# The first group of gates in a hybrid encoder block: four turned-sum transfers, one gate product and three scale sums issued at other places

## The chip, the core and the metric

One core of one Trainium2 chip runs the whole layer. The metric is the device time of one execution in microseconds (us), lower is better; the time before is the median of three runs. The core's engines work at the same time and meet through semaphores: PE multiplies matrices, ACT, DVE and POOL work on vectors, and SP issues the transfers.

## The reference

The layer takes 1024 tokens of width 1024. What matters here is how the attention's output and the gates meet:

```
u = RMSNorm(x)
[q|k|v|cB|cC|cH|gA|gB] = u @ W_in
A: 2-D neighbourhood attention, 8 heads x 64
B: cB * conv3(cC * cH)
m = sigmoid(gA) * (A @ W_A) + sigmoid(gB) * (B @ W_B)
x = x + m @ W_o
x = x + relu(RMSNorm(x) @ W1)^2 @ W2
```

The inputs are float32. The kernel splits each operand of a product into two float16 parts, high and low, and adds three products of parts for each one of the reference.

## The kernel before

**Stages.** The program is one straight list of instructions per engine, made by a Python program that writes them in the order in which each engine shall take them. After the norm and the projections to v, q and k comes the attention, a loop over steps `k` of 0 to 79 (lines 1138 to 1180), with the projections of the convolution branch written between its matmuls (`emit`). Then come eight groups of gates (lines 1401 to 1524), then the product with W_o and the MLP.

**Attention.** A step `s` is one head of one block of 128 queries. Its scores come in step `k = s`, its softmax weights P are split into a high and a low part on ACT (line 1085) and DVE (line 1089), and for each pair of heads SP turns P with one transposing DMA into a tile `PT` (`at_turn`, line 1094, issued in step `k = s + 6`). Every eighth step PE multiplies four turned pairs with v (`at_pv`, line 1106). The last of these comes in step 73 and uses the pair that is turned in step 68.

**Gates.** A group of gates is a product of u with 256 columns of W_in, done with one level of Strassen's scheme: seven products of sums of u's quarters (the "forms" 0 to 6) with sums of the weights' quarters. Each product is 12 matmuls of 128x128 weights and 128x512 columns (four blocks times three pairs of parts), so one product counts as 6144 columns in `work`. The pairs of parts come as high times high, high weights times low form, low weights times high form. In this text "product three" is the entry 3 of `SEVEN`, which takes form 6. The forms' sums were computed early and stored to DRAM as `gs`; SP reads them back with transposing DMAs (`turn_one`, line 1133), one for each block `n` of 128 tokens and each part `s`. Forms 4 and 5 go into places of `qD` that the attention no longer reads, and are turned during the attention, at steps listed in `turns`. Form 2 (into `uT`) and form 6 (into `s4T`) follow after the attention loop (line 1209 and on), eight transfers each.

**The first group** (`first_gate`) is written out by hand: gate products 1, 2, 6, 4, 7, 5, 3 with the four products of the two branches (`branch(g, half)`, 12 matmuls each; branch 0 is A, branch 1 is B) between them. A `then` that is handed to `unit` is the work on ACT and DVE after a product; it is written behind the next product's matmuls.

**Weights of a gate group** are made ready one group ahead, by `prep_s(n + 1)` while group `n` runs: rows scaled on ACT (line 1242), squares summed (line 1251), sums of quarters on POOL (line 1256), then one scale for the whole chunk. For this scale PE adds the partitions with one matmul against `ones` (line 201, `all_sum`), DVE makes a power of two out of it in some small instructions (lines 204 and 435 to 442), and ACT (line 1276) and DVE (line 1272) write the high and low parts in four pieces: the quarter 11, the quarters of row 2, and two pieces out of the tile `gsum`. Gate product six of the next group, its second, uses the last of them. How many products PE runs between the sum of squares and the matmul against `ones` is set by the third argument of `scale_of`. In this text "chunk five" is the weights of group five, made ready while group four runs.

**Work between PE products** is written with `tick`, which advances these generators by one step, so a matmul against `ones` that moves also moves the small DVE instructions behind it against the other DVE work.

Of the kernel before, what the change touches and what calls it, by code (L numbers as in the profile page):

```python
# [52 lines left out]
def encoder_block(ctx: ExitStack, tc: tile.TileContext, x, weights, cols, gqk, rel, masks, out):  # L53
# [25 lines left out]
    sc = base.tile([128, 600], F32, name="sc")  # L79
# [41 lines left out]
    def advance(g):  # L121
        try:
            return next(g) or True
        except StopIteration:
            return False

    def step(n=1):
        for _ in range(n):
            for g in list(fg):
                if not advance(g):  # L130
                    fg.remove(g)

    def tick(n=1):

        for _ in range(n):
            i = 0
            while i < len(bg):
                r = advance(bg[i])
                if not r:
                    bg.pop(i)  # L140
                elif r == WAIT and side[0]:
                    i += 1
                else:
                    break
# [3 lines left out]
    def spend(v=0, a=0):  # L148

        debt[0] += v  # L150
        debt[1] += a
# [55 lines left out]
    def unit(mms, post=None, steps=0, ticks=0, free=False):  # L207

        for ps, l, r, a, b in mms:
            T.matmul(ps, l, r, start=a, stop=b, skip_group_check=free)  # L210
        for g in list(hooks):
            if not hold[0] and not advance(g):
                hooks.remove(g)
        units[0] += 1
        work[0] += len(mms) * mms[0][0].shape[-1]
        settle()
        if post:
            late.append(post)
        for i in range(max(steps, ticks)):
            if i < steps:  # L220
                step()
            if i < ticks:
                tick()

    def settle():
        while late:
            late.pop(0)()
# [117 lines left out]
    for (kind, j), pieces in plan():  # L345
        ch = chunks[kind, j] = Chunk(kind, [(nk, sum(n for _, n in cs)) for _, _, nk, cs in pieces],
                                     {"A": "wa", "B": "wb"}.get(kind, "ws"), rows.get(kind, lambda j: g1)(j),
                                     j if kind == "V" else None, 9 if kind in "VQKCS" else 0)
# [115 lines left out]
    def group(ps, pairs):  # L464
        return [(ps, l, r, i == 0, i == len(pairs) - 1) for i, (l, r) in enumerate(pairs)]
# [6 lines left out]
    def ch_mms(ps, act, half, ch, nk, w, c):  # L472

        return group(ps, [(ch.parts[:, sw, k * w + c:k * w + c + 128], act(sa, k)[:, half * 512:half * 512 + 512])
                          for k in range(nk) for sw, sa in PASSES])
# [656 lines left out]
    def turn_one(i, f, n, s):  # L1132
        SP.dma_start_transpose(FORM[f](s)[:, :, 128 * n:128 * n + 128], GS[:, n, (3, 0, 2, 1)[i], s])  # L1133

    turns = {}
    for n in range(8):
        turns[35 + 2 * n] = (1, 4, n // 2, n % 2)
        turns[51 + 2 * n if n < 4 else 65 + 2 * (n - 4)] = (2, 5, n % 4, n // 4)

    def emit(n):  # L1140
        for ps, l, r, a, b in islice(conv, n):
# [3 lines left out]
    for k in range(N + 16):  # L1145
        p, w = k // 16, k % 16
        if p < 3 and w == 3:
            bias[p + 1] = bias_load(p + 1)
        if p < 3 and w in (12, 14):
            bias_make(*bias[p + 1], (w - 12) // 2)  # L1150
            spend(550)
        ok = lambda d: 0 <= k - d < N
        debt[:] = [max(0, v - SPAN) for v in debt]
        spend(1200 if k > 4 else 600, 1120 if k > 3 else 500)
        if ok(0):
            at_qk(k)
        emit(0 if k > 13 and k % 8 == 1 else 4)
        if ok(1):
            at_max(k - 1)
        if ok(4):  # L1160
            at_hi(k - 4)
        if k % 2 and ok(3):
            at_recip(k - 3)
        if ok(5):
            at_lo(k - 5)
        if k % 2 == 0 and ok(6):
            at_turn(k - 6)
        if k in turns:
            turn_one(*turns[k])
        if ok(1):  # L1170
            at_exp(k - 1)
        units[0] += 1
        conv_step(1)
        for _ in range(3):
            if k < 2 or not room() or not fill():
                break
        emit(3 if k < 12 else 0 if k % 8 == 1 else 4 if k % 8 in (3, 5, 7) and k > 16 else 5)
        if k % 8 == 1:
            for d in (17, 15, 13, 11):
                if ok(d):  # L1180
                    at_pv(k - d)
        if ok(14 + k % 2):
            at_out(k - 14 - k % 2, k % 2)
# [16 lines left out]
    p3 = ExitStack()  # L1200
# [25 lines left out]
    def scale_of(am, more, n=3, lag=1):  # L1226

        a, mark = am
        yield from apart(mark, n * 6144, work)
        b, s, inv = cols_of("prep", 1), cols_of("prep", 1), keep()  # L1230
        yield from all_sum(a, b, anybank(), 1e-36, lag)
        yield from pow2_half(b, 14, s, inv, more)
        return s, inv
# [11 lines left out]
    def forms_sum(ch, t, gap):  # L1245

        sm = cols_of("prep", 2)
        for i in range(2):
            while len(ch.raw) <= i:
                yield WAIT  # L1250
            A.activation(t[:, 2:4].rearrange("p a c -> p (a c)"), ch.raw[i], AF.Square, accum_out=sc[:, at(sm, i)])
            yield
        ch.r = [ch.raw[i].rearrange("p (n m) -> p n m", n=2) for i in range(2)]
        (w11, w12), (w21, w22) = ([r[:, 0], r[:, 1]] for r in ch.r)
        for o, a, b in ((0, w11, w12), (1, w12, w22), (2, t[:, 0], w22), (3, t[:, 2], w21)):
            G.tensor_tensor(t[:, o], a, b, op=OP.add)  # L1256
        yield from apart(work[0], gap * 6144, work)
        ch.sum = sum_of(sm)
        yield
# [30 lines left out]
    def prep_s(n):  # L1290

        ch = cS[n]
        t = w3p.tile([128, 4, 512], F32, name="gsum", bufs=1)
        yield from rows_scaled(ch, g1)
        yield from forms_sum(ch, t, 2 - 0 * (n % 2 == 0))
        s, ch.inv = yield from scale_of(ch.sum, 9, 2 + 1*(n % 2 == 0), 0)
        hold[0] = True
        while done[0] < ch.first:
            yield WAIT
        ch.P = wsp.tile([128, 7, 2, 512], F16, name="w16_s", tag="ws")  # L1300
        yield from forms_split(ch, t, s, ch.P)
        ch.split = True
        hold[0] = False
# [82 lines left out]
    def first_gate(post):  # L1386

        sg = w3p.tile([128, 4, 512], F32, name="sg")
        z = [sg[:, i] for i in range(4)]
        P, iv, ps = cS[0].P, cS[0].inv, {}  # L1390

        def op(o, a, b, less=False):
            V.tensor_tensor(z[o], ps[a], z[b], op=OP.subtract if less else OP.add)

        def sigmoid(i):
            A.activation(z[i], z[i], AF.Sigmoid, scale=sc[:, iv])

        def p6():
            op(1, 6, 1)

        def p2():
            op(0, 2, 1)
            sigmoid(0)

        def p7():
            op(3, 7, 1)
            op(2, 4, 3)
            sigmoid(2)

        def p5():  # L1410
            op(3, 5, 3, True)
            sigmoid(3)
            op(1, 5, 1, True)

        def p3():
            op(1, 3, 1)
            sigmoid(1)

        def gate_of(i, then=None):
            f, w = SEVEN[i]  # L1420
            ps[i] = anybank()
            unit(group(ps[i], [(P[:, w, sw, k * 128:k * 128 + 128], actS(f, sa, k))
                               for k in range(4) for sw, sa in PASSES]), then, 2, 4)

        def branch(g, half):
            ch, act = ((cA[0], actA), (cB[0], actB))[g]
            built(ch)
            bk = anybank()
            unit(ch_mms(bk, act, half, ch, 4, 256, 0), lambda: post(g, half, bk, sc[:, ch.inv], sg), 2, 4)

        gate_of(1, lambda: A.activation(z[1], ps[1], AF.Copy))
        gate_of(2, p2)
        gate_of(6, p6)
        gate_of(4)
        branch(0, 0)
        gate_of(7, p7)
        branch(0, 1)
        gate_of(5, p5)
        branch(1, 1)
        gate_of(3, p3)  # L1440
        branch(1, 0)

    def branch_units(n, post):
        j, cc = n // 2, (n % 2) * 128
# [7 lines left out]
    for n in range(8):  # L1452
# [5 lines left out]
        if n < 7:  # L1458
            sg = gate_units(n) if n else None
# [7 lines left out]
            def post(g, half, ps, iv, sg=sg, m=m):  # L1467
                t = sg[:, 2 * half + g]
                V.scalar_tensor_tensor(t, ps, iv, t, op0=OP.mult, op1=OP.mult)
                if g == 1:  # L1470
                    V.tensor_tensor(m[:, half], sg[:, 2 * half], t, op=OP.add)
# [629 lines left out]
    later = {}  # L2101
# [147 lines left out]
    for n in range(28):  # L2249
        s, o = n // 7, n % 7  # L2250
# [3 lines left out]
        for j in range(4):  # L2254
            bk = anybank()
# [87 lines left out]
```

## Time and profile before

| what | value |
|---|---|
| runs of before | 1196.51, 1197.23 and 1197.74 us, median 1197.23 |
| the profiled execution's own time | 1197.15 us |
| its span on the core | 1195.2 us |
| granted clock of PE, mean | 0.999 |
| PE busy | 1183.5 us, 99% of the span |
| DVE busy | 966.6 us, 81% |
| ACT busy | 760.6 us, 64% |
| POOL busy | 416.2 us, 35% |

The span is the time between the first and the last instruction of the execution; 1197.15 - 1195.2 = 1.95 us of the profiled time lie outside it. In the timeline a row gives its start in us, its length, the engine, the line of the program, the operation, the tiles it writes and reads, how many instructions it merges (x), and in brackets the idle time of the engine ahead of it with what ended it. Matmuls overlap in the records, by some 0.16 us, so the step from the start of one product to the start of the next is what PE spends on it.

### The profile page before, as it was taken

To read this page: it belongs to the slowest core of one execution; us is meant where nothing else is said; L and a number is where in the kernel's file an instruction comes from. 1 tells how busy PE (TensorE), PEld (TensorE's weight loads), DVE (VectorE), ACT (ScalarE), POOL (GpSimd) and SP (SyncE) were. 2 spreads that over 40 slices of the span, in tenths; PEclk is the share of its full clock that TensorE was granted. 3 is DMA by queue.
4 is the path that set the end of the run, shared out by engine and by line. 5 is a ranking of instruction groups with operands and counts; after the bars stand their busy time and mean duration, and the time that the engine had idled before them with its cause. 6 is when DMAs were issued, how large, how long until landed. Compare 5 with 4: busy or idle time off the path is not lost.

```text
span 1195.2 us, 16991 instructions
## 1 busy us (share of the span) xinstructions
PE 1183.5 (99%) x6253; PEld 579.5 (48%) x6253; DVE 966.6 (81%) x1665; ACT 760.6 (64%) x1181; POOL 416.2 (35%) x288
## 2 busy tenths in 40 slices
PE   8999999999999999999999999999999999999998
PEld 6444445555444444444467445555444444444444
DVE  6799888899668686868886867766749899998997
ACT  7866578786657776436766576666686743646440
POOL 2640012224321222001012475776873431324193
PEclk9999999999999999999999999999999999999999
DMA  9949457766625454233364444533675927244302
GB/s 291 217 158 205 114 126 138 141 149 108 188 83 184 150 176 141 89 144 138 87 153 148 161 176 176 193 129 133 207 255 202 375 74 259 94 142 192 106 36 106
DMA packets 181283, 189.61 MB, mean 159 GB/s; under 512 B 138192, under 2 KB 138704, under 8 KB 177104
## 3 DMA queue, kind: packets, MB, share of 16 engines
q1 hardware_dynamic: 181200, 188.52, 52.1%
q8 instruction: 49, 0.80, 0.3%
q14 instruction: 34, 0.28, 0.1%
HBM read 117.19 MB, written 37.75 MB: 130 GB/s over the span
## 4 chain that ended last, share of the span: by engine, by line
PE 57%; issue 6%; POOL 5%; DMA 4%; DVE 2%; ACT 1%; SPq 1%; DVEq 0%; POOLq 0%; ACTq 0%
PE ps_s L210 21%; PE ps_d L210 21%; PE ps_o L210 14%; POOL tsum L1651 3%; DMA hs<-as 3%; POOL as L1539 2%; SPq L1133 1%; PE ps_d L1142 1%; DVE w L1272 1%; DVE as L1989 0%; ACT raw L1642 0%; ACT as L1912 0%; DMA PT<-P 0%; ACT w L1276 0%; DMA s4T<-gs 0%
## 5 line engine op out<-in xcount | busy, mean ns | idle before, releaser
L210 PEld LDWEIGHTS <-ops 128*128 128x128 f16 x1356 | 132.5, 98 | 157.3
L210 PEld LDWEIGHTS <-w 128*128 128x128 f16 x1272 | 124.3, 98 | 127.1 <-issue 0.2
L1142 PE MATMUL ps_d<-uT,w_ws 128*128 128x512 f16 x528 | 123.7, 379 | 0.0
L210 PE MATMUL ps_d<-ops 128*128 128x512 f16 (+1 forms) x540 | 121.0, 374 | 0.0
L1539 POOL TENSOR_TENSOR as<-as 128x512 f32<-128x512 f32 x56 | 92.0, 1644 | 73.8 <-ACT as L1914 70.8
L210 PE MATMUL ps_s<-ops 128*128 128x512 f16 x504 | 115.6, 379 | 0.0
L2166 ACT ACTIVATE ops<-hf,sc 128x2048 f16<-128x2048 f32 x26 | 52.0, 2000 | 86.0 <-PE ps_d L210 37.5
L210 PEld LDWEIGHTS <-w_s 128*128 128x128 f16 x672 | 65.3, 98 | 79.0 <-issue 0.9
L210 PEld LDWEIGHTS <-uT 128*128 128x128 f16 x528 | 51.4, 98 | 62.0
L1651 POOL TENSOR_TENSOR tsum<-raw 128x512 f32<-128x512 f32 x28 | 40.5, 1463 | 114.7 <-ACT raw L1642 114.7
L1142 PEld LDWEIGHTS <-w_ws 128*128 128x128 f16 x528 | 51.4, 98 | 54.2
L210 PE MATMUL ps_o<-ops 128*128 128x512 f16 x312 | 71.6, 379 | 0.0
L2168 DVE SCALAR_TENSOR_TENSOR ops<-hf,sc,ops 128x2048 f16<-128x2048 f32 x26 | 68.0, 2617 | 3.6 <-ACT ops L2166 3.5
L1256 POOL TENSOR_TENSOR gsum<-raw 128x512 f32<-128x512 f32 x14 | 18.6, 1338 | 125.8 <-ACT raw L1242 125.8
L1272 DVE SCALAR_TENSOR_TENSOR w<-tsum,sc,w 128x1024 f16<-128x1024 f32 x28 | 46.8, 1679 | 14.5 <-ACT w L1276 14.5
L210 PE MATMUL ps_d<-u2T,w 128*128 128x512 f16 (+1 forms) x276 | 58.2, 360 | 0.0
L210 PE MATMUL ps_s<-u2T,w 128*128 128x512 f16 (+1 forms) x252 | 54.0, 364 | 0.0
L1272 DVE SCALAR_TENSOR_TENSOR w<-raw,sc,w 128x1024 f16<-128x1024 f32 (+1 forms) x20 | 28.2, 1418 | 31.7 <-ACT w L1276 31.7
L1072 ACT ACTIVATE sz<-sz,sc 128x384 f32<-128x384 f32 (+1 forms) x64 | 37.2, 581 | 24.3 <-DVE sc L1063 15.8
L1912 ACT ACTIVATE as<-as 128x2048 f32<-128x2048 f32 (+1 forms) x18 | 30.9, 1718 | 31.3 <-DVE as L1989 18.8
L309 ACT ACTIVATE w_ws<-raw,sc 128x512 f16<-128x512 f32 (+1 forms) x64 | 37.2, 654 | 18.2 <-DVE sc L282 18.2
L210 PE MATMUL ps_s<-u2x,w 128*128 128x512 f16 (+1 forms) x228 | 48.5, 362 | 0.0
(430 smaller groups left out, 2692.2 us busy)
## 6 DMA issues: line engine op xcount, KB each, us to landing
raw<-in_weights SPq DMA_DIRECT2D x97, 512.0 KB, 4.8
hs<-as SPq DMA_DIRECT2D x16, 1792.0 KB, 8.3
hf<-hs SPq DMA_DIRECT2D x26, 1024.0 KB, 5.9
w2x<-in_weights SPq DMA_DIRECT2D x16, 512.0 KB, 7.0
raw<-in_weights SPq DMA_DIRECT2D x16, 384.0 KB, 4.0
mL<-in_weights SPq DMA_DIRECT2D x10, 512.0 KB, 4.7
mH<-in_weights SPq DMA_DIRECT2D x9, 512.0 KB, 4.3
xt<-in_x SPq DMA_DIRECT2D x8, 512.0 KB, 8.2
```

The lines of the kernel that those rows point to most:

```text
L210: T.matmul(ps, l, r, start=a, stop=b, skip_group_check=free)
L309: A.activation(self.parts[:, 0, f + o:f + o + m], self.raw[p][:, o:o + m], AF.Copy, scale=sc[:, c:c + 1])
L1072: A.activation(z, z, AF.Exp, scale=-1.0, bias=sc[:, d["mx"]], accum_out=sc[:, d["sm"]])
L1133: SP.dma_start_transpose(FORM[f](s)[:, :, 128 * n:128 * n + 128], GS[:, n, (3, 0, 2, 1)[i], s])
L1142: T.matmul(ps, l, r, start=a, stop=b)
L1256: G.tensor_tensor(t[:, o], a, b, op=OP.add)
L1272: V.scalar_tensor_tensor(o(1), w, sc[:, s], o(0), op0=OP.mult, op1=OP.subtract)
L1539: sub.tensor_tensor(z[o], z[a], z[b], op=op)
L1651: G.tensor_tensor(t[:, o], a, b, op=OP.add)
L1912: A.activation(v[:, 0:4], v[:, 0:4], AF.Relu)
L2166: A.activation(P[:, 1, 0], hf, AF.Copy, scale=sc[:, Rs])
L2168: V.scalar_tensor_tensor(P[:, 1, 1], hf, sc[:, Rs], P[:, 1, 0], op0=OP.mult, op1=OP.subtract)
```

## The change

```diff
     turns = {}
     for n in range(8):
-        turns[35 + 2 * n] = (1, 4, n // 2, n % 2)
-        turns[51 + 2 * n if n < 4 else 65 + 2 * (n - 4)] = (2, 5, n % 4, n // 4)
+        turns.setdefault(35 + 2 * n, []).append((1, 4, n // 2, n % 2))
+        turns.setdefault(51 + 2 * n if n < 4 else (65, 65, 69, 70)[n - 4], []).append((2, 5, n % 4, n // 4))
...
-        if k in turns:
-            turn_one(*turns[k])
+        for tn in turns.get(k, ()):
+            turn_one(*tn)
...
-        yield from forms_sum(ch, t, 2 - 0 * (n % 2 == 0))
-        s, ch.inv = yield from scale_of(ch.sum, 9, 2 + 1*(n % 2 == 0), 0)
+        yield from forms_sum(ch, t, 2 - 0 * (n != 3))
+        s, ch.inv = yield from scale_of(ch.sum, 9, 2 + 1*(n != 3), 0)
...
-        def branch(g, half):
+        def branch(g, half, later=None):
             ch, act = ((cA[0], actA), (cB[0], actB))[g]
             built(ch)
             bk = anybank()
-            unit(ch_mms(bk, act, half, ch, 4, 256, 0), lambda: post(g, half, bk, sc[:, ch.inv], sg), 2, 4)
+            fin = lambda: post(g, half, bk, sc[:, ch.inv], sg)
+            unit(ch_mms(bk, act, half, ch, 4, 256, 0), None if later else fin, 2, 4)
+            return fin
...
         branch(1, 1)
-        gate_of(3, p3)
-        branch(1, 0)
+        fin = branch(1, 0, True)
+        gate_of(3, lambda: (p3(), fin()))
```

There are three edits. The last four transfers of form 5 were issued in steps 65, 67, 69 and 71 and are now issued in steps 65, 65, 69 and 70. In the first group, product three now stands behind the last branch product, and that branch product's own work on DVE stands behind product three's. In `prep_s` the distance from the squares to the matmul against `ones` becomes three products for chunks one, five and seven, where it was two; chunk three keeps two, and the even chunks keep three. The edit of the argument of `forms_sum` multiplies by 0 and changes nothing.

On SP, at the end of the attention, the difference reads as follows; `P_3219` is the pair of step 60, `P_3314` (now `P_3315`) the last pair, and the `qD` rows are transfers of form 5.

```order
 L1094 DMA_TRANSPOSE PT<-P_3126 128x12x128
 L1094 DMA_TRANSPOSE PT<-P_3175 128x12x128
-L1133 DMA_TRANSPOSE qD<-gs 128x4x128
+L1133 DMA_TRANSPOSE qD<-gs 128x4x128 x2
 L1094 DMA_TRANSPOSE PT<-P_3219 128x12x128
-L1133 DMA_TRANSPOSE qD<-gs 128x4x128
-L1094 DMA_TRANSPOSE PT<-P_3314 128x8x128
+L1094 DMA_TRANSPOSE PT<-P_3315 128x8x128
 L1133 DMA_TRANSPOSE qD<-gs 128x4x128 x2
 L1133 DMA_TRANSPOSE uT<-gs 128x4x128 x4
```

One form-5 transfer moves from between the last two turned P to ahead of both. Everything behind the last P keeps its order, and the number of transfers is the same.

On PE, behind the first branch-B product (`ps_o<-bT`), before:

```order
L210 LDWEIGHTS w_wb
L210 MATMUL ps_o<-bT,w_wb 128x512
L210 LDWEIGHTS w_s
L210 MATMUL ps_d<-s4T,w_s 128x512
L210 LDWEIGHTS w_s
```

and now, at the same place:

```order
L210 LDWEIGHTS w_wb
L210 MATMUL ps_o<-bT,w_wb 128x512
L210 LDWEIGHTS w_wb
L210 MATMUL ps_d<-bT,w_wb 128x512
L210 LDWEIGHTS w_wb
```

The first reading of `s4T` on PE comes 12 matmuls later. Further ahead on PE, chunk one's matmul against `ones` moves from the front to the back of the second branch-A product.

On DVE, while group four runs, from the scale of chunk five to the last low parts of its weights, before (line 1469 scales a branch product, line 1471 adds two):

```order
L204 TENSOR_SCALAR sc<-ps_o 128x1
L435 TENSOR_SCALAR sc<-sc 128x1
L437 TENSOR_SCALAR sc<-sc 128x1
L1469 SCALAR_TENSOR_TENSOR sg<-ps_s,sc,sg 128x512
L439 TENSOR_SCALAR sc<-sc 128x1
L441 TENSOR_SCALAR sc<-sc 128x1
L442 TENSOR_SCALAR sc<-sc 128x1
L1272 SCALAR_TENSOR_TENSOR w_s<-raw,sc,w_s 128x512
L1469 SCALAR_TENSOR_TENSOR sg<-ps_d,sc,sg 128x512
L1272 SCALAR_TENSOR_TENSOR w_s<-raw,sc,w_s 128x2x512
L1272 SCALAR_TENSOR_TENSOR w_s<-gsum,sc,w_s 128x2x512 x2
```

and now (the two lines are 1471 and 1473 in the changed kernel, and the first branch product's scaling stands ahead of these rows):

```order
L204 TENSOR_SCALAR sc<-ps_d 128x1
L435 TENSOR_SCALAR sc<-sc 128x1
L437 TENSOR_SCALAR sc<-sc 128x1
L1471 SCALAR_TENSOR_TENSOR sg<-ps_o,sc,sg 128x512
L439 TENSOR_SCALAR sc<-sc 128x1
L441 TENSOR_SCALAR sc<-sc 128x1
L442 TENSOR_SCALAR sc<-sc 128x1
L1272 SCALAR_TENSOR_TENSOR w_s<-raw,sc,w_s 128x512
L1471 SCALAR_TENSOR_TENSOR sg<-ps_s,sc,sg 128x512
L1473 TENSOR_TENSOR m<-sg 128x512
L1272 SCALAR_TENSOR_TENSOR w_s<-raw,sc,w_s 128x2x512
L1272 SCALAR_TENSOR_TENSOR w_s<-gsum,sc,w_s 128x2x512 x2
```

The chunk's scale waits for one branch product more, and the third branch product's scaling and sum now stand ahead of the last three pieces of the split.

## The prediction, made before the changed kernel ran

> **What bounds the kernel now.** I read the waits of PE first, then the busy time by window, then the timelines of PE, SP and DVE around the change. The waits of PE (engine, line, tile, what it waited for, us, times, longest) are five rows in all; the first stands at the very start of the program, the second in the change's region:
>
> ```profile
> PE ps_o L574 <- DMA xt<-in_x: 4.6, 1, 4.6
> PE ps_o L1106 <- DMA PT<-P: 1.2, 1, 1.2
> ```
>
> The busy time by window (PE is the column behind the comma) says how little is left: 1.86 us are idle in one window and 0.55 in the next.
>
> ```profile
> 250.00:300.00 50.00, 48.14 (x459) 26.04 (x458) 46.14 (x114) 35.48 (x81) 19.41 (x21) 1.00 0.71 131
> 300.00:350.00 50.00, 49.45 (x232) 22.27 (x231) 31.72 (x76) 28.20 (x49) 14.38 (x13) 1.00 0.43 127
> ```
>
> So PE sets the end, and a change pays only by what it takes from PE's gaps. The timeline of PE shows three of them:
>
> ```profile
> 299.04 0.53 PE L1106 MATMUL ps_o<-PT,vT 128*64 128x128 f16 x12 [1.21 <-DMA PT<-P]
> 299.50 2.76 PE L210 MATMUL ps_s<-uT,w_s 128*128 128x512 f16 x12
> ...
> 309.87 0.17 PE L201 MATMUL ps_d<-ones 128*128 128x1 bf16 x1
> ...
> 315.36 0.16 PE L201 MATMUL ps_s<-ones 128*128 128x1 bf16 x1
> ...
> 323.15 0.38 PE L210 MATMUL ps_d<-s4T,w_s 128*128 128x512 f16 x1
> 323.95 2.53 PE L210 MATMUL ps_d<-s4T,w_s 128*128 128x512 f16 x11 [0.43 <-DMA s4T<-gs]
> 326.32 1.03 PE L210 MATMUL ps_s<-bT,w_wb 128*128 128x512 f16 x4
> ```
>
> A product takes (309.87 - 299.50) / 4 = 2.59 us, a matmul 0.216. First gap: 1.21 us ahead of the last turned P, which PE wanted at 299.04 - 1.21 = 297.83. Second: from the one matmul against ones to the next are 5.49 us for two products, 5.49 - 5.18 - 0.03 (the matmul itself) = 0.28 too many. Third: product three takes 326.32 - 323.15 = 3.17, 0.58 too many; it waits behind its first matmul for the low part of s4T. All that can be won here is 1.21 + 0.28 + 0.58 = 2.07 us.
>
> **The transfers.** SP and the two low parts of P that release its last turns on DVE:
>
> ```profile
> 288.35 1.98 SPq L1133 DMA_TRANSPOSE qD<-gs  x1
> 292.00 1.45 SPq L1094 DMA_TRANSPOSE PT<-P  x1
> 293.52 1.62 SPq L1133 DMA_TRANSPOSE qD<-gs  x1
> 295.25 1.24 SPq L1094 DMA_TRANSPOSE PT<-P  x1
> ...
> 299.22 5.76 SPq L1133 DMA_TRANSPOSE uT<-gs  x4
> ...
> 311.94 10.38 SPq L1133 DMA_TRANSPOSE s4T<-gs  x8
> ```
>
> ```profile
> 291.02 0.61 DVE L1089 SCALAR_TENSOR_TENSOR P<-sz,sc,P 128x384 f16<-128x384 f32 x1
> ...
> 292.74 0.87 DVE L1089 SCALAR_TENSOR_TENSOR P<-sz,sc,P 128x256 f16<-128x256 f32 x2
> ```
>
> SP stood idle from 288.35 + 1.98 = 290.33 to 292.00, until P came (291.63 on DVE, 0.37 later SP). The moved transfer fits there: issued at 290.4, it takes 1.62 by the nearest row, at most 1.98, and is off SP by 292.0 to 292.4. The turn of step 60 slips by 0 to 0.4. The last turn needs its P at 292.74 + 0.87 = 293.61, so it goes at 293.61 + 0.37 = 293.98 in place of 295.25: 1.27 earlier. From issue to landing (medians of two narrow windows, and the last s4T transfer in the chain of waits):
>
> ```profile
> PT<-P SPq DMA_TRANSPOSE x1, 3.7
> ...
> PT<-P SPq DMA_TRANSPOSE x1, 4.6
> ...
> 321.06 2.75 DMA s4T<-gs
> ```
>
> 3.7 is that very transfer, so it lands at 297.7, when PE wants it: I take the gap as closed. By 4.6, the other row, it lands at 298.6 and 0.4 of the gap is won. But PE does not keep 1.21. Its next meeting is the matmul against ones for the first branch-B weights, whose operand DVE makes here:
>
> ```profile
> 308.92 0.16 DVE L331 CAST ones<-sc 128x1 bf16<-128x1 f32 x1
> ...
> 315.14 0.16 DVE L1223 CAST ones<-sc 128x1 bf16<-128x1 f32 x1
> ```
>
> The cast ends at 309.08, and the second shows what a wait costs: ending at 315.30, it let PE go at 315.36. DVE's work before 308.92 hangs on the convolution's tail, not on PE's products, and its order is unchanged. PE would be there at 309.87 - 1.21 = 308.66 and now waits until 309.14. Of the first gap remain 309.87 - 309.14 = **0.73 us** (bounds 0 and 1.21).
>
> **The matmul against ones of chunk one** moves behind the second branch-A product, 2.59 later, where its cast of 315.30 is long done: **0.28 us** won (bounds 0 and 0.28). Behind it, DVE's split of chunk one comes later; the row of its last low part and the chain's row of the product that reads it:
>
> ```profile
> 326.77 1.28 DVE L1272 SCALAR_TENSOR_TENSOR w_s<-gsum,sc,w_s 128x1024 f16<-128x1024 f32 x1
> ...
> 331.67 2.59 PE ps_d L210 x12
> ```
>
> The high-by-high and high-by-low matmuls come first, so the low part is wanted 0.43 after 331.67. It ends at 328.05: 4.05 to spare. PE comes 1.6 earlier and DVE up to 2.59 later if nothing else moves, which would be 0.1 late; but two of the posts that stood between the pieces now stand behind them, and the loads on SP and so the squares come about 1.3 earlier. I take 0.
>
> **Product three** is read 2.59 later on PE, about 325.74 - 1.01 = 324.73, while the last s4T transfer landed at 323.81 even where it stood, and SP, solid from 299.22 on, now runs 1.3 ahead. The whole **0.58** is won (bounds 0.43, the wait that the row names, and 0.58). The branch product's post stands behind product three's; DVE does both as before. That costs nothing, since product six of the next group only needs the split.
>
> **Chunk five**, with the same later matmul against ones, has no such room. PE, DVE, ACT and POOL while group four runs, and one sum (line 1471) away from POOL:
>
> ```profile
> 435.28 0.17 PE L201 MATMUL ps_o<-ones 128*128 128x1 bf16 x1
> ...
> 445.67 1.67 PE L210 MATMUL ps_o<-qD,w_s 128*128 128x512 f16 x7
> ```
>
> ```profile
> 435.52 0.16 DVE L204 TENSOR_SCALAR sc<-ps_o 128x1 f32<-128x1 f32 x1 [0.45 <-PE ps_o L201]
> ...
> 437.13 0.75 DVE L1469 SCALAR_TENSOR_TENSOR sg<-ps_s,sc,sg 128x512 f32<-128x512 f32 x1 [1.08 <-ACT sg L1347]
> 437.80 0.14 DVE L439 TENSOR_SCALAR sc<-sc 128x1 int32<-128x1 int32 x1
> 437.98 0.15 DVE L441 TENSOR_SCALAR sc<-sc 128x1 int32<-128x1 int32 x1
> ...
> 438.92 0.75 DVE L1272 SCALAR_TENSOR_TENSOR w_s<-raw,sc,w_s 128x512 f16<-128x512 f32 x1 [0.73 <-ACT w_s L1276]
> ...
> 440.25 1.28 DVE L1272 SCALAR_TENSOR_TENSOR w_s<-raw,sc,w_s 128x1024 f16<-128x1024 f32 x1
> 441.44 2.48 DVE L1272 SCALAR_TENSOR_TENSOR w_s<-gsum,sc,w_s 128x1024 f16<-128x1024 f32 x2
> ...
> 444.62 1.26 DVE L1471 TENSOR_TENSOR m<-sg 128x512 f32<-128x512 f32 x1
> ...
> 501.69 0.69 DVE L1471 TENSOR_TENSOR m<-sg 128x512 f32<-128x512 f32 x1
> ```
>
> ```profile
> 438.17 1.76 ACT L1276 ACTIVATE w_s<-raw,sc 128x512 f16<-128x512 f32 x2
> ...
> 444.05 2.96 POOL L1256 TENSOR_TENSOR gsum<-raw 128x512 f32<-128x512 f32 x2 [23.22 <-ACT raw L1242]
> ```
>
> Before, the split ends at 441.44 + 2.48 = 443.92, and its last low part is wanted at 445.67 + 0.43 = 446.10: 2.18 to spare. Now, in times of this trace: the matmul at 437.87, DVE's first step 0.24 later at 438.11, two steps of 0.19, the post (0.67 by 437.13 to 437.80), the step to the scale (0.18): 439.41, against 437.98. ACT starts 0.19 behind it, DVE's first low part 0.75 behind that, at 440.35. Then come 0.67, the third branch product's post and sum, 0.78 (as 1471 follows 1469 elsewhere) and 0.61, the three low parts with 1.19 + 2.48: 446.08. That meets the 446.10 with nothing left; with the hand-over of 0.06 and a weight load I take a stall of **0.15** (bounds 0 and 2.3). For the upper one the whole 2.59 and a post and sum of 0.67 + 1.26 are late, 4.52 - 2.18. The sum is short, 0.61, only because it now stands ahead of POOL's additions, which start when the split frees gsum (444.05 behind 443.92); beside them it took 1.26 against 0.69.
>
> The Trainium skill, GPSIMD Engine Reference, section Specifications, says that POOL shares its SBUF interfaces with DVE and that DVE instructions with two SBUF inputs contend with it; the two rows of line 1471 agree (1.26 against 0.69).
>
> Chunk seven's weights come into use behind four more products of the last group, 10.4 us, so its 2.6 lie in cover.
>
> Sum against the profiled 1197.15: 0.73 + 0.28 + 0.58 - 0.15 = 1.44, so 1195.7; the median of the runs lies 0.08 higher: **1195.8 us**.
>
> **The rivals.** (1) The cast is no bound, or DVE reaches it sooner: 2.07 - 0.15 = 1.92 won, 1195.3. For it: DVE is idle several times before 308.92; against it: those idles end with POOL and ACT work of the convolution. (2) The last turn, now close behind other transfers, lands by the row of 4.6: 0.4 + 0.28 + 0.58 - 0.15 = 1.1 won, 1196.1; for it the spread of 3.7 to 4.6, against it that fewer transfers are in flight ahead of it than before.
>
> The Trainium skill, DMA: Bandwidth & Descriptors, section Issuing engines are not separate DMA queues, says that all transfers end on the same 16 engines and interleave there, so two issued together would delay each other; this is the second rival, and the rows of 3.7 and 4.6 bear it out in part.
>
> (3) The other side: chunk five's split is late by more than I count, at product six of group five. From a stall of 1.6 on it eats everything; with 2.3, 1197.23 - 1.59 + 2.34 = 1198.0, and if its last three pieces run beside POOL at the ratio 1.26 / 0.69, 3 us more, 1201. For it: nothing to spare in my sum; against it: POOL waits for the split's end. (4) The change doesn't do what it says: the last turn still goes at 295.25, since its P or the moved transfer is late. Then 0.28 + 0.58 - 0.15 = 0.71, 1196.5.
>
> **How the numbers follow.** Forecast 0.52, rival (1) 0.16, (2) 0.14, (3) 0.14, (4) 0.04. A change of 0.2%, 2.4 us, is about what a measurement can tell from none. More than that is won only with all gaps closed and luck in the runs, which differ by 1.2: half of rival (1) and 0.06 of the forecast, 0.14. Slower by it is most of (3), 0.10. The rest, 0.76, is within. The range goes from 1194.7 (rival (1) with 0.6 of spread) to 1197.6 (the mild end of rival (3)); the forecast's own is 1195.2 to 1196.4.
>
> **What would show it.** Right: no wait of PE on PT or s4T; the wait at the branch-B matmul against ones, some 0.5 us; product one of group one at 327.3 in place of 328.91; a gap of 0.1 to 0.3 in product six of group five, behind its second matmul. Wrong: PE's next products still 1.2 ahead behind the cast, a gap of 1 us or more in group five or in product six of group one, or any new wait of PE elsewhere.

## The result and the profile after

The changed kernel takes 1195.72 us (median of 22 runs, 1195.15 to 1196.58), the kernel before beside it 1197.43 us (22 runs, 1196.51 to 1199.52). The ratio is 0.9986, with a 95% interval of 0.998 to 0.9992. So 1.7 us are won, a gain that the interval tells from none, and less than the 0.2% that the prediction counts as a change. The profiled execution took 1195.5 us, its span is 1193.4 us.

The waits of PE after the change (engine, line, tile, what it waited for; us in total, times, longest):

```profile
PE ps_o L574 <- DMA xt<-in_x: 4.5, 1, 4.5
PE ps_s L1049 <- DVE sc L1063: 0.7, 2, 0.5
PE ps_d L201 <- DVE ones L331: 0.5, 1, 0.5
...
PE ps_d L546 <- DVE ones L609: 0.2, 1, 0.2
```

The wait for `PT` is gone and no wait for `s4T` is there. A new one of 0.5 us stands at a matmul against `ones`, for the cast of line 331. The row of 0.2 us at line 546, also new, stands at the very start of the program, where the executions scatter (last section). The windows of before, now (PE busy behind the comma):

```profile
250.00:300.00 50.00, 49.34 (x466) 26.56 (x464) 46.13 (x114) 35.49 (x81) 19.41 (x21) 1.00 0.74 134
300.00:350.00 50.00, 49.50 (x233) 22.33 (x232) 32.28 (x77) 29.95 (x51) 14.41 (x13) 1.00 0.44 124
```

The first window gains 49.34 - 48.14 = 1.20 us of work, the second only 0.05: gaps have closed in it, but the new wait at 309 stands in it too. The timeline of PE tells more:

```profile
285.58 2.03 PE L1106 MATMUL ps_o<-PT,vT 128*64 128x128 f16 x66
...
296.07 2.03 PE L1106 MATMUL ps_o<-PT,vT 128*64 128x128 f16 x66
...
305.81 2.75 PE L210 MATMUL ps_s<-uT,w_s 128*128 128x512 f16 x12
309.06 0.18 PE L201 MATMUL ps_d<-ones 128*128 128x1 bf16 x1 [0.50 <-DVE ones L331]
...
314.28 2.75 PE L210 MATMUL ps_s<-qD,w_wa 128*128 128x512 f16 x12
316.87 0.17 PE L201 MATMUL ps_d<-ones 128*128 128x1 bf16 x1
...
324.67 2.75 PE L210 MATMUL ps_s<-s4T,w_s 128*128 128x512 f16 x12
327.26 2.75 PE L210 MATMUL ps_o<-uT,w_s 128*128 128x512 f16 x12
```

The 66 value matmuls run without a stop, and product three (`s4T`) takes one step of 2.59. The only long step is the one ahead of the branch's matmul against `ones`: 309.06 - 305.81 = 3.25, which is 0.66 too many.

The **stretch** that the rest of this text measures goes from the value products of step 65 (285.58) to product one of group one (327.26). It is 41.68 us, and was 328.91 - 285.64 = 43.27: 1.59 us less. Behind it, to PE's last group, nothing is won. These are that group's rows, before and after:

```profile
1188.01 2.78 PE L210 MATMUL ps_d<-ops 128*128 128x256 f16 x24
```

```profile
1186.39 2.78 PE L210 MATMUL ps_d<-ops 128*128 128x256 f16 x24
```

From product one of group one to there are 859.10 us before and 859.13 after. SP and the two casts on DVE, after:

```profile
292.01 3.14 SPq L1094 DMA_TRANSPOSE PT<-P  x2
...
303.90 1.47 SPq L237 DMA_DIRECT2D raw<-in_weights  x3
...
310.73 10.38 SPq L1133 DMA_TRANSPOSE s4T<-gs  x8
```

```profile
308.85 0.16 DVE L331 CAST ones<-sc 128x1 bf16<-128x1 f32 x1
...
313.83 0.16 DVE L1223 CAST ones<-sc 128x1 bf16<-128x1 f32 x1
```

The two turned P now go out together, and all behind them on SP runs 1.2 us sooner: `s4T` at 310.73 in place of 311.94, chunk one's weights (`raw`) at 303.90 in place of 305.09 (the row of before is shown further below). The cast of the branch weights stands where it stood, 308.85 against 308.92.

### The profile page after: what moved, and what is told of

It is laid out like the page before. It is cut to its first block, busy times and chain, and to the rows that moved or that the text cites. A ratio compares the mean times of both kernels' runs of the same rounds, so it can differ in the third digit from the quotient of the medians.

```text
span 1193.4 us, 16991 instructions
## 1 busy us (share of the span) xinstructions
PE 1183.0 (99%) x6253; PEld 579.1 (49%) x6253; DVE 965.9 (81%) x1665; ACT 760.7 (64%) x1181; POOL 416.3 (35%) x288
## 4 chain that ended last, share of the span: by engine, by line
PE 71%; DVE 3%; issue 1%; POOL 1%; ACT 1%; DVEq 0%; POOLq 0%; ACTq 0%
PE ps_s L210 27%; PE ps_d L210 26%; PE ps_o L210 19%; POOL tsum L1653 1%; DVE P L1089 1%; POOL cv L908 0%; DVE w L1272 0%; DVE sz L1063 0%; DVE as L1991 0%; DVE w_wa L300 0%; DVE sc L320 0%; ACT w L1276 0%; ACT as L1914 0%; POOL z L905 0%; DVE cv L891 0%
```

## The experiments

Seven more kernels ran, four of them twice, and the changed kernel once more: twelve runs, each with one trace (the expectations call a trace a look). Where no number of runs is given, the time is of a single execution. Single times do not tell the parts apart, since executions of one kernel differ by 1 us and more. What tells them apart is the stretch and where it is longer than the bare work. The bare work is 41.00 us: one of the kernels below ran the stretch without any gap. Gaps are read from the steps between PE rows, as above, so they are a little longer than the waits in brackets: the wait for the last turned P is 1.21 in its bracket, but takes 1.40 out of PE's steps. All traces, in us; a "sum" stands for the matmul against `ones` of the weights named, and "landing" goes from the first issue of chunk one's weights on SP to ScalarE's start on them:

| kernel | last turned P | branch-B sum | chunk one's sum | product three | stretch | landing |
|---|---|---|---|---|---|---|
| before | 1.40 | 0 | 0.28 | 0.58 | 43.27 | 3.83 |
| the change | 0 | 0.66 | 0 | 0 | 41.68 | 3.70 |
| the change, again | 0.07 | 0.62 | 0 | 0 | 41.70 | 3.75 |
| turns alone | 0.01 | 0.63 | 0.66 | 0.08 | 42.39 | 4.42 |
| product three alone | 1.08 | 0 | 1.38 | 0 | 43.47 | 4.55 |
| the same, again | 0.86 | 0 | 0.54 | 0 | 42.41 | 4.02 |
| sums alone | 1.07 | 0 | 0 | 1.52 | 43.59 | 4.07 |
| the same, again | 1.01 | 0 | 0 | 1.56 | 43.57 | 4.06 |
| turns and product three | 0.25 | 0.41 | 0.43 | 0 | 42.09 | 4.26 |
| the same, again | 0.01 | 0.68 | 0 | 0 | 41.70 | 3.89 |
| the change, cast early | 0.33 | 0 | 0 | 0 | 41.33 | 4.12 |
| the same, again | 0 | 0 | 0 | 0 | 41.00 | 4.13 |

The two kernels that change only the sums of chunks five and three have the stretch of the whole change, 41.68 and 41.70, with landings of 4.29 and 4.02.

### The turns alone

```diff
-        turns[51 + 2 * n if n < 4 else 65 + 2 * (n - 4)] = (2, 5, n % 4, n // 4)
+        turns.setdefault(51 + 2 * n if n < 4 else (65, 65, 69, 70)[n - 4], []).append((2, 5, n % 4, n // 4))
```

Expected:

> Of the change only the moved transfers of form 5. Read on PE: the distance from the start of step 65's value products to the start of product one of group one, 43.27 us before, 41.68 in the changed kernel. Theory (each gap has its own cause, and the loads that follow the transfers on SP also pull the cast of 315.30 forward): first gap 0.5 in place of 1.21, seen at the branch-B matmul against ones; second gap closed although its matmul is not moved; product three waits some 0.3 for s4T, which lands 1.27 earlier while PE comes 1.01 earlier. Distance 42.0. Rival (the second gap needs its matmul moved): 0.2 to 0.3 stay ahead of chunk one's matmul against ones, and product three waits about as much less.

It took 1196.2 us. PE's rows at the two matmuls against `ones` and at product three:

```profile
309.08 0.18 PE L201 MATMUL ps_d<-ones 128*128 128x1 bf16 x1 [0.46 <-DVE ones L331]
...
311.70 2.75 PE L210 MATMUL ps_d<-qD,w_s 128*128 128x512 f16 x12
314.95 0.16 PE L201 MATMUL ps_s<-ones 128*128 128x1 bf16 x1 [0.49 <-DVE ones L1223]
...
322.74 2.83 PE L210 MATMUL ps_d<-s4T,w_s 128*128 128x512 f16 x12
325.41 2.75 PE L210 MATMUL ps_s<-bT,w_wb 128*128 128x512 f16 x12
```

The wait for P is gone and 0.63 of it comes back at the branch's cast, as the prediction had it. On SP, the last transfers that product three needs:

```profile
311.01 10.38 SPq L1133 DMA_TRANSPOSE s4T<-gs  x8
```

Two things were not expected. Chunk one's sum lost 0.66, although its weights were issued 1.0 us sooner than before (304.09 against 305.09). They landed later: 4.42 us from issue to use in place of 3.83. And product three, left where it was, loses only 325.41 - 322.74 - 2.59 = 0.08. That is not the turns' doing alone: PE came to it 0.66 later than it would have without the loss at the sum. What is left waits for the last transfers of `s4T`. In the three traces whose rows show PE waiting for them (the kernel before and the sums alone), product three's second matmul starts 11.97 to 12.05 us behind the first issue of `s4T` on SP (323.95 - 311.94 = 12.01 before). Here this issue comes 25.40 us behind the value products of step 65, and 26.30 before. So the stretch is 0.88 shorter because `s4T` goes out 0.90 sooner, where 1.27 was expected of both; by this reading, a punctual sum would only have made PE wait 0.7 at product three.

### Product three alone

```diff
-        gate_of(3, p3)
-        branch(1, 0)
+        fin = branch(1, 0, True)
+        gate_of(3, lambda: (p3(), fin()))
```

(`branch` also gets its argument `later` from the change.) Expected, first run:

> Of the change only product three behind the last branch product. Theory: product three's gap of 0.58 goes, the other two stay: 1.21 ahead of the last turned P and 0.28 ahead of chunk one's matmul against ones. Distance 42.69 in place of 43.27. Rival (the branch product's work on DVE, now behind product three's, delays group one): 43.0 or more, with a wait of PE in group one.

It took 1197.52 us, and the stretch was 0.20 longer than before, not 0.58 shorter. Product three has no gap. The loss is at chunk one's sum, which this edit does not touch. ScalarE's first row on chunk one's weights, and PE's, in this kernel:

```profile
309.90 1.70 ACT L1242 ACTIVATE raw<-raw,sc 128x256 f32<-128x256 f32 x4 [2.97 <-DMA raw<-in_weights]
```

```profile
316.33 0.16 PE L201 MATMUL ps_s<-ones 128*128 128x1 bf16 x1 [1.22 <-DVE ones L1223]
```

and the same for the kernel before, SP first:

```profile
305.09 1.47 SPq L237 DMA_DIRECT2D raw<-in_weights  x3
```

```profile
308.92 1.70 ACT L1242 ACTIVATE raw<-raw,sc 128x256 f32<-128x256 f32 x4 [2.16 <-DMA raw<-in_weights]
```

The loads go out at 305.35 here and are used at 309.90, 4.55 later, against 3.83 before. The whole chain behind (squares, cast, matmul against `ones`) moves with them. Of the 1.38 - 0.28 = 1.10 that the gap has grown, 0.72 is this; most of the rest is that PE lost less at the last turned P (1.08 in place of 1.40) and so came sooner. Whether the late landing was chance could only be told by a second run:

> Product three behind the last branch product, alone, once more. Theory: the move does take product three out of the landing of s4T (0.58), and what the first look lost again was chunk one's weights, which landed late by chance: the wait at chunk one's matmul against ones is about the time from the first issue of these loads to ScalarE's start, less 3.5 (0.28 at 3.83 before, 1.22 at 4.55). The stretch from step 65's value products to product one of group one (43.27 before) is then 42.7 if that time is 3.8, and 43.4 if it is 4.5. Rival: the move is worth nothing whatever the landing, and the stretch is 43.3 or more even at 3.8.

This time the landing is 4.02, the gap at chunk one's sum 0.54 and the stretch 42.41, below the 42.7 to 43.4 that were expected and 0.86 shorter than before: 0.58 at product three, 0.54 at the last turned P (0.86 in place of 1.40), which this edit does not touch, less 0.26 at chunk one's sum (0.54 in place of 0.28). Over 11 runs the median is 1197.32 us, the ratio 0.9995 (0.9986 to 1.0004). So the edit does take the 0.58 out at product three in both traces, but what the execution as a whole gains is no more than the scatter of the two landings ahead of it.

### The sums alone

```diff
-        s, ch.inv = yield from scale_of(ch.sum, 9, 2 + 1*(n % 2 == 0), 0)
+        s, ch.inv = yield from scale_of(ch.sum, 9, 2 + 1*(n != 3), 0)
```

Expected, first run:

> Of the change only the later matmuls against ones of chunks one, five and seven. Theory: 0.28 is won ahead of chunk one's matmul and given back at product three, whose s4T lands when it did: its gap grows from 0.58 to 0.86. Distance 43.27 as before, no gain. Product six of group five loses 0.02 to 0.05. Rival (the parts simply add up): 42.99.

It took 1197.53 us. Chunk one's sum has no gap, but product three has:

```profile
319.88 2.75 PE L210 MATMUL ps_o<-bT,w_wb 128*128 128x512 f16 x12
322.95 0.38 PE L210 MATMUL ps_d<-s4T,w_s 128*128 128x512 f16 x1 [0.32 <-issue]
324.21 2.53 PE L210 MATMUL ps_d<-s4T,w_s 128*128 128x512 f16 x11 [0.88 <-DMA s4T<-gs]
326.58 2.75 PE L210 MATMUL ps_s<-bT,w_wb 128*128 128x512 f16 x12
```

The two steps around it are 3.07 and 3.63, together 1.52 too many, where 0.58 were before. PE is sooner at product three by the 0.28 that it no longer waits at the sum and by 0.33 that it waits less at the last turned P. It then waits for `s4T` instead, whose issue on SP (312.16) comes no sooner than before: 26.58 us behind the value products, against 26.30.

```profile
312.16 10.38 SPq L1133 DMA_TRANSPOSE s4T<-gs  x8
```

Second run:

> The sums later, alone, once more. Theory: the wait at chunk one's matmul against ones is gone, but what it gives up goes into the wait for s4T at product three, which comes earlier by as much (0.58 before, 1.2 in the first look); the stretch stays at 43.1 to 43.6, and the time at 1197.4 to 1197.7, ratio 0.9995 to 1.0005. Rival: without the other two edits the term of 0.28 is there all the same: stretch 43.0 or less and ratio 0.9993 or less.

Again 1.56 at product three, stretch 43.57, median 1197.49 us, ratio 0.9998 (0.9989 to 1.0007). The theory holds: alone, this edit wins nothing. Product six of group five takes 2.62 and 2.63 in the two traces, against 2.59 before, so 0.03 to 0.04 are lost there, as expected.

### Turns and product three, without the sums

This kernel is the change with the old argument of `scale_of`. Expected, first run:

> The change without the later matmuls against ones: transfers and product three alone. Theory: all of the change's gain, since the earlier loads already take chunk one's cast out of PE's way: distance 41.7, no gap of 0.1 or more ahead of chunk one's matmul, and no loss in product six of group five. Rival: 0.28 missing, 41.96.

1197.64 us; 1.6 of it were lost ahead of the stretch, which starts at 287.20 in place of 285.58 (more on that below). The stretch is 42.09, neither the 41.7 of the theory nor quite the 41.96 of its rival: chunk one's sum lost 0.43 at a landing of 4.26. Second run:

> Turns and product three, without the sums, once more. Theory: all three waits of before are gone except the one at chunk one's matmul against ones, and that is the time from the first issue of chunk one's loads to ScalarE's start less 3.85 (0.42 at 4.26 in the first look), none where they land in 3.7: the stretch is 41.7 at 3.7 and 42.4 at 4.55, and the median over many executions 0.2 to 0.5 above the whole change, 1196.0 to 1196.3. Rival: the sums are worth nothing, 41.7 and 1195.8.

```profile
309.60 0.18 PE L201 MATMUL ps_d<-ones 128*128 128x1 bf16 x1 [0.52 <-DVE ones L331]
...
314.81 0.17 PE L201 MATMUL ps_s<-ones 128*128 128x1 bf16 x1
```

At a landing of 3.89 chunk one's sum costs nothing at all, and the stretch is 41.70, the same as with the whole change. The formula for the single trace holds (3.89 less 3.85), but the forecast for the median does not: 1195.80 us over 11 runs, ratio 0.9987 (0.9978 to 0.9996), so no 0.2 to 0.5 above the whole change. In the median nothing is left for the sums that these runs could show. What they buy is that chunk one's sum had no gap in any of the 8 traces that have them, while it had 0, 0.43 and 0.66 in the three that have the turns without them.

### The branch's cast ahead of the splits

If 0.66 us is left at the branch's matmul against `ones`, and its cast on DVE stands behind four splits of other weights, the cast can go first. Two more steps of its generator are taken, and one more product lies in between so that PE's order stays as it is (ScalarE makes one copy later, behind chunk one's scaling):

```diff
-            yield from apart(units[0], 3 if self.kind != "O" else 1 + (self is cO[1]))
+            yield from apart(units[0], 4 if self is cB[0] else 3 if self.kind != "O" else 1 + (self is cO[1]))
...
+    for _ in range(2):
+        advance(bg[-1])
```

Expected, first run and second:

> The change, and with it the three small VectorE instructions that end in the cast of the branch's second sum (L102, L329, L331) ahead of the four w_wa splits (L300) instead of behind them. If what is left of the first gap is this cast alone (0.50 at the branch's matmul against ones), that wait is gone, the stretch of the PE from step 65's value products to product one of group one (43.27 before, 41.68 with the change) is 41.1 to 41.3, and the time is about 1195.2, ratio to before about 0.9982. Rival: the gap is shut by something else next (the sum's own readiness, chunk one's cast), the stretch stays at 41.6 to 41.8 and the time at 1195.7.

> The change with the branch's cast ahead of the splits, once more. Theory: the wait of 0.5 at the branch's matmul against ones is gone in every execution, so the ratio to before is 0.9978 again to 0.0005 and the stretch 41.1 to 41.4 (41.33 in the first look, 0.33 of it a late last turn of P). Rival: the first look was luck, the ratio is 0.9985 or above.

The changed kernel ran beside the first (below, "once more"). First run: 1195.16 us over 11 runs, against 1195.84 for the change in the same comparison; ratio to before 0.9978 (0.997 to 0.9987). Second: 1195.51 us, ratio 0.9982 (0.9973 to 0.9991). DVE and PE in the second trace:

```profile
305.16 0.16 DVE L331 CAST ones<-sc 128x1 bf16<-128x1 f32 x1
```

```profile
286.52 2.03 PE L1106 MATMUL ps_o<-PT,vT 128*64 128x128 f16 x66
...
306.75 2.75 PE L210 MATMUL ps_s<-uT,w_s 128*128 128x512 f16 x12
309.34 0.17 PE L201 MATMUL ps_d<-ones 128*128 128x1 bf16 x1
...
327.52 2.75 PE L210 MATMUL ps_o<-uT,w_s 128*128 128x512 f16 x12
```

The cast is done 4 us before PE wants it, the step ahead of the matmul is 2.59, and the stretch is 327.52 - 286.52 = 41.00, all of it work. So by the traces this version beats both kernels, the change by 41.68 - 41.00 = 0.68 us here and by 41.68 - 41.33 = 0.35 in the first trace. The medians agree in sign: 0.68 below the change in the comparison that has both, and 0.2 to 0.3 below its two medians (1195.72 and 1195.84) in the other; the intervals of the ratios still overlap. The rival, that something else shuts the gap, is out: no wait stands at the branch's matmul against `ones` in either trace. In the first of them the last turned P came 0.33 late, so that transfer is the next bound there.

### The change once more

> The change once more, unaltered. If the stretch from step 65's value products to product one of group one is set by the program, it is 41.68 again to 0.1, and the ratio to before 0.9986 to 0.0004. Rival: the landing of chunk one's weights, which differed by 0.8 between the looks so far (3.70 to 4.55 from the first issue to ScalarE's start), sets it; then it differs from 41.68 by up to 0.5. With the sums a product later there are 2.4 of room at chunk one's matmul against ones, so the first is expected.

Stretch 41.70, median 1195.84 us over 11 runs, ratio 0.9991 (0.9982 to 1.0). The stretch came out as expected. The ratio is 0.0005 above the first, a little over the 0.0004 that was allowed, while the changed kernel's two medians differ by 0.12 us; the intervals overlap.

### Chunk five's sum one product later still

```diff
-        s, ch.inv = yield from scale_of(ch.sum, 9, 2 + 1*(n != 3), 0)
+        s, ch.inv = yield from scale_of(ch.sum, 9, 2 + 1*(n != 3) + (n == 5), 0)
```

> The change, with chunk five's matmul against ones moved one product further back, so that one product in place of two lies between it and product one of group five. If VectorE's chain of splits behind it is what decides there (the last split ends at 444.40 now, where product six's second part wants it at 444.44), the chain ends 2.0 to 2.6 later and the products one and six of group five lose 2.0 to 2.6 together (steps of 2.59 and 2.61 now). Rival: the chain has slack that isn't seen (VectorE takes the splits ahead of its other work), and less than 1.0 is lost.

First the whole change, PE and then DVE's last split:

```profile
441.42 2.75 PE L210 MATMUL ps_s<-uT,w_s 128*128 128x512 f16 x12
444.01 2.78 PE L210 MATMUL ps_o<-qD,w_s 128*128 128x512 f16 x12
446.62 2.75 PE L210 MATMUL ps_d<-uT,w_s 128*128 128x512 f16 x12
```

```profile
441.93 2.47 DVE L1272 SCALAR_TENSOR_TENSOR w_s<-gsum,sc,w_s 128x1024 f16<-128x1024 f32 x2
```

Product six of group five takes 446.62 - 444.01 = 2.61 in place of 2.59. The split ends at 441.93 + 2.47 = 444.40, and the first matmul that reads its last part comes at 444.01 + 0.43 = 444.44. With the sum one product later, PE:

```profile
441.87 2.75 PE L210 MATMUL ps_d<-bT,w_wb 128*128 128x512 f16 x12
445.07 0.60 PE L210 MATMUL ps_s<-uT,w_s 128*128 128x512 f16 x2 [0.45 <-ACT w_s L1276]
445.85 2.33 PE L210 MATMUL ps_s<-uT,w_s 128*128 128x512 f16 x10 [0.18 <-DVE w_s L1272]
448.18 0.61 PE L210 MATMUL ps_o<-qD,w_s 128*128 128x512 f16 x2
449.82 2.33 PE L210 MATMUL ps_o<-qD,w_s 128*128 128x512 f16 x10 [1.03 <-DVE w_s L1272]
451.98 0.38 PE L210 MATMUL ps_d<-uT,w_s 128*128 128x512 f16 x1
```

From 441.87 to 451.98 are three products in 10.11 us, 2.34 more than three steps of 2.59: as expected (2.0 to 2.6). The execution took 1200.68 us, but 3.0 us of it were lost ahead of the stretch, which starts at 288.62 in place of 285.58, and have no part in this.

### Chunk three's sum later as well

```diff
-        s, ch.inv = yield from scale_of(ch.sum, 9, 2 + 1*(n != 3), 0)
+        s, ch.inv = yield from scale_of(ch.sum, 9, 3, 0)
```

> The change, with chunk three's matmul against ones moved back as well, as for all other chunks. The last split of chunk three ends at 385.22 now and is wanted about 387.36. One product later it would end 2.1 to 2.6 later, at 387.3 to 387.8: a stall of 0 to 0.45 at the second product of group three, 0.1 taken, so no change of the time that can be seen, and the landing of chunk three's sum has no part in it. Rival: the splits collide with VectorE's other work there and 0.5 or more is lost.

```profile
387.57 2.79 PE L210 MATMUL ps_d<-qD,w_s 128*128 128x512 f16 x12
390.19 2.75 PE L210 MATMUL ps_s<-uT,w_s 128*128 128x512 f16 x12
```

The product of group three that is read here takes 2.62, 0.03 too many, and the execution took 1196.14 us. So chunk three behaves like chunk five did under the change: 0.03 lost, which no time of an execution can tell. Leaving it at two products saves no more than these 0.03.

## Why the prediction was right

**The bound and the first term.** The prediction said that closing the wait for P (1.21) would win only 0.73, because PE would then meet the cast of the branch weights on DVE. The table has 1.40 of gap before and 0.66 after, so 0.74 won. The gap itself was mis-sized: by the steps it is 1.40 and not the 1.21 of its bracket, so 2.26 in place of 2.07 could be won in all, and the kernel with the early cast won 43.27 - 41.00 = 2.27. The term of 0.73 does not suffer from this, since it was taken from the time of the cast. The kernel with the early cast shows that this cast is the whole of what held PE there: with it moved, the gap is gone and nothing else takes its place. Rival (1), that the cast is no bound, is out: the wait was there in every trace with the turns and without the early cast. Rival (4) is out too: both last turns were off SP by 292.01 + 3.14 = 295.15, and before the second was only begun at 295.25.

**Rival (2)**, a last turn that lands by the row of 4.6, did not come. A late last turn showed in three of the traces with the turns, with 0.07, 0.25 and 0.33 us. In the first two it costs nothing, because the cast is there as a second bound: 0.07 + 0.62 and 0.25 + 0.41 are again the 0.66 to 0.69. The cover is gone only with the cast moved.

The last two turned P of the changed kernel, issued one behind the other, in the view of the tile `PT` from 293.3 to 294.6 (time from issue to landing):

```profile
DMA to landing us min/median/max: 3.7/3.7/3.8
```

So the pair did not slow down: 3.7 was also the last turn's time before, and in the other traces with the turns it is 3.1 to 4.0, not the 4.6 of the rival. The late ones in the two kernels with 0.25 and 0.33 were issued later, some 1.9 us ahead of the convolution's matmul against `ones` in place of 2.4, and landed in 3.7. There the two form-5 transfers ahead of them had kept SP for 4.12 and 4.19 us, against 3.61 in the first trace of the change. So the moved transfer can delay the turn of step 60 by 0.6 to 0.7, beyond the 0 to 0.4 that the prediction allowed, and the last turn with it.

The Trainium skill, DMA: Bandwidth & Descriptors, section Issuing engines are not separate DMA queues, says that transfers share the same 16 engines and interleave there, which gave this rival its reason; these landings show no price of it for two turned P issued together.

**Chunk one's sum** was given 0.28, with the cause that the matmul moves behind a cast at a fixed time. The size came out in the sum, but the step is wrong in two ways. The cast's time is not fixed: it follows the landing of chunk one's weights, which is 3.70 to 4.55 us over these traces, and the gap without the later sums, which also depends on how early PE comes, is anything from 0 to 1.38. And the gain is not the edit's own. In the trace of the changed kernel the cast ended at 313.99, while at its old place the matmul would have been wanted at 314.28, so the gap was closed in that execution without the edit. The prediction used the loads' being 1.3 sooner only for the split, not here. That the term of 0.28 fits is the luck of one trace.

**Product three** was given 0.58 as its own gain. All traces with the edit have no gap there, so the total is right. But the sums alone make it 1.52, and the turns alone leave 0.08 of it, with 0.66 lost just ahead. The three terms of the prediction are not separate prices; they are one chain in which PE, let go at one place, waits at the next. Their sum is right because the change makes all three places punctual at once, but for the cast: 0.73 + 0.28 + 0.58 = 1.59 forecast, 43.27 - 41.68 = 1.59 measured. Chunk one's landing has little part in this sum. Before, the last wait is the one for `s4T`, 12.0 us behind its issue, and what PE loses ahead of that at the sum it waits less there. After, the last wait is the one for the cast, which starts 23.25 to 23.30 us behind the value products in every trace in which PE waits for it.

No kernel has the turns and the sums without product three's move. An estimate from the rows: `s4T` goes out at 310.73 in the change, so its last part is there at 310.73 + 12.0 = 322.7. At its old place product three would start at 322.08 and want it 0.22 later, and wait some 0.4; at the new one it wants it at 324.67 + 0.22 = 324.89, with 2 us to spare.

**Chunk five.** The stall at product six of group five was put at 0.15 with bounds 0 and 2.3; it is 0.02 to 0.03, so this term was mis-sized by 0.12. The steps to the scale add up to 439.34, not to the 439.41 that is written, which changes little. PE is 1.66 ahead here (444.01 against 445.67), and with that the split ends at 444.40 + 1.66 = 446.06, against the 446.08 that were forecast. What was too much is the surcharge for a hand-over and a weight load. The forecast of DVE's order held: the splits come ahead of POOL's additions, and the sum of two branch products that stands between them takes 0.69.

```profile
440.12 0.69 DVE L1473 TENSOR_TENSOR m<-sg 128x512 f32<-128x512 f32 x1
...
445.10 1.26 DVE L1473 TENSOR_TENSOR m<-sg 128x512 f32<-128x512 f32 x1
```

The Trainium skill, GPSIMD Engine Reference, section Specifications, has POOL and DVE on shared SBUF interfaces, so that a DVE instruction with two SBUF inputs contends with POOL. The two rows agree: 0.69 ahead of POOL's additions, which start at 444.53, and 1.26 beside them.

The place is as tight as the sum said, 0.04 us to spare on paper; the kernel with one product more shows what lies behind, 2.34, so rival (3) named a real cliff that the change stops just short of. It lost this because the whole chain came a product later; that splits beside POOL's additions would cost 3 us more was not seen in any run, since POOL's additions start only behind the last split (444.53 behind 444.40). Chunk seven cost nothing that shows: from product one of group one to PE's last group only the 0.03 of chunk five are lost.

**The time.** 1.44 us were forecast, 1.71 are the difference of the medians and 1.59 - 0.03 = 1.56 what the trace shows on PE. The rest is within the interval of the ratio. Chunk one's split cost nothing, as taken. Of the 0.27 between the gain forecast and the gain of the medians, 0.12 is chunk five's surcharge.

## What to carry to other kernels

When one gap on the bounding engine is closed, look for the next thing this engine meets, and price the gap by the difference; several gaps on one chain are not several prices, and an edit that closes one of them alone may win nothing. A gap that hangs on a transfer has no fixed size: read it in several executions before an edit is credited with it. Before a wait is attacked at its transfer, look at what stands ahead of the small instruction that ends it: here three tiny DVE instructions behind four splits held PE for 0.66 us, where the whole change won 1.7.

## What the runs showed of the hardware

The same three loads, issued from the same queue at nearly the same place, were used 3.70 to 4.55 us behind their first issue, in fourteen traces; the spread of 0.85 us is three times the gap of 0.28 that the prediction took as given.

The start of the program scatters more. DVE needs the second part of the first weights there; in the changed kernel and in the one with chunk five's sum later still it reads:

```profile
7.38 1.36 DVE L602 TENSOR_REDUCE sc<-raw 128x2 f32<-128x512 f32 x2 [0.45 <-DMA raw<-in_weights]
```

```profile
8.91 1.33 DVE L602 TENSOR_REDUCE sc<-raw 128x2 f32<-128x512 f32 x2 [2.02 <-DMA raw<-in_weights]
```

That start was 1.5 us later, with nothing changed ahead of it. PE then waited 2.1 us in place of 0.2 for its first matmul against `ones`, and came to the stretch 3.0 us later. One such execution costs more than the change wins, which is why the parts were read from the stretch and not from single times. Why these loads land so differently stays open; no run here tried it.
